# Query and key projections of two attentions: 512 weight columns a product, one norm for both

## Chip, cores and metric

One Trainium2 chip, one core. The metric is the time of one execution on the device, in microseconds (us), from three timed runs of the kernel before. The profile is of one further execution.

## What is computed

Two layers of a trunk, for 128 context tokens and 512 latent tokens that share all weights. In each layer a modulated RMS norm is followed by one input projection `z = h @ w_in` of 1024 features to 2560 columns, which are cut into eight parts:

```python
    lx, lg, nq, nk, nv, dq, dk, dv = in_projection(h, p['w_in'])      # 512, 512, then six of 256
    ya, sf, sb = lru_bidir(dwconv_centred(lx, ...), lg, p, zeros, zeros)
    q = rms_norm(nq.reshape(b, t, 4, 64), p['na_q_norm']) * 64 ** -0.5
    k = rms_norm(nk.reshape(b, t, 4, 64), p['na_k_norm'])
    q2 = rms_norm(dq.reshape(b, t, 4, 2, 32), p['df_q_norm'])
    k2 = rms_norm(dk.reshape(b, t, 4, 2, 32), p['df_k_norm'])
    y = jnp.concatenate([ya, merge_heads(yb), merge_heads(yc)], axis=-1) @ p['w_out']
```

`ya` is a bidirectional linear recurrence (LRU) on `lx`, gated by `lg`. `yb` is the neighbourhood attention (NA): 4 heads of 64, a window of 8 rows and 16 columns of the latent grid and 128 cached context keys; the context tokens attend among themselves. `yc` is the differential attention (DF): 4 heads of two components of 32, with rope on the latent tokens and cached keys as well. A norm over each head stands between projection and attention for all four of `nq`, `nk`, `dq`, `dk`. A convolutional feed-forward network closes the layer. Keys and values of the context tokens are outputs too.

## The kernel before, in words

All 640 tokens are handled at once: the modulated activations lie in `h`, features on partitions, as two tiles of rounded float32 (a high and a low part), and every weight is split in the same two parts on its way in. A product of two such numbers takes three matmuls: high by high, high by low, low by high (`mm3`, lines 269 to 274).

The weights pass three stations. `wload` (L361 to 365) brings 1 MB into one of two tiles of 2048 columns ("raw"), which the loads of the adaLN weights (`adaw`, 1 MB each, L196) share. `unit` (L372 to 378) splits half of it: ScalarE copies the high part (`wh`, L110), VectorE subtracts for the low part (`wl`, L117), 1024 columns each. The units lie in a ring of four (`ring`, L77), which the weights of the LRU (`lx` groups, and `gw0`) use first. A list `jobs` (L727 to 733) has the loads in order; `prep` (L735) does the next one, `take` (L739) hands out the oldest that is ready.

The attention projections have tokens on the output's partitions. `tok_chunk` (L817) takes one job of 8 x 256 weights, so two units, and goes over the five token tiles two at a time: a PSUM tile of 512 columns (`m`, three of them, L81) gets 256 columns for each of two token tiles, 24 products each. After the first two tiles it calls `prep` for the next chunk, and after each group one step of the adaLN generator `ada` (a load of 1 MB and four small products at L203). `normed_chunk` (L829) does so for a q or k: ScalarE copies the PSUM tile into `z` and squares it in place (L835), VectorE sums per head (L836). When all five tiles are through, `rsqrt` (L119) works out the inverse root by nine small VectorE operations behind two more, with 20 numbers a partition in NA and 40 in DF, and one multiplication scales `z` (L841).

The order in the program is `na_q`, `na_k`, the chunk of v, `na_prompt` and `na_sample` (attention of NA), `df_k`, `df_q`, the chunk of DF's v, then DF's scores (L1034 to 1048). `df_qk` (L891) adds gain and rope: four products on POOL (L905), a multiplication (L908) and a sum (L909) on VectorE. `df_k` then makes "stacks" of the keys (`stack`, L912): ScalarE and VectorE write high and low parts four times side by side, four transposes on TensorE (L920), copies into `ks`. DF's scores read these (L1079).

The order in which engines get their instructions is fixed when the program is built: a scheduler takes, at each simulated moment, the ready instruction of the best priority, which is its place in the program unless `later(n)` shifts it. It also gives out the buffers. Each engine then runs its own list in order and waits on semaphores. So a chunk of projections that stands behind `na_sample` in the program runs as filler while that waits for its softmax.

The job that a layer's mixer begins with is loaded earlier (`first`, L428 in layer 0, `job_load(l + 1)` at L1497 for layer 1).

Of the kernel before, what the change touches and what calls it, by code (L numbers as in the profile page):

```python
# [68 lines left out]
def trunk_kernel(ctx: ExitStack, tc: tile.TileContext, A, O):  # L69
# [26 lines left out]
    def m_tile():  # L96
        return ps_m.tile([P, 512], F32, tag="m", name="m")
# [10 lines left out]
    def copy(eng, out, in_):  # L108
        if eng == "a":
            return nc.scalar.activation(out, in_, AF.Copy)  # L110
        elif eng == "v":
            nc.vector.tensor_copy(out, in_)
        else:
            nc.gpsimd.tensor_copy(out, in_)
# [1 line left out]
    def sub(out, a, b, eng=None):  # L116
        (eng or nc.vector).tensor_tensor(out, a, b, op=OP.subtract)  # L117

    def rsqrt(v, n, name="rs"):  # L119
        yi = tiny.tile([P, max(n, 3)], I32, tag=f"yi{max(n, 3)}", name=name, bufs=2)[:, :n]  # L120
        nc.vector.tensor_scalar(yi, v.bitcast(I32), -0.5, float(0x5F3759DF), op0=OP.mult, op1=OP.add)
        y = yi.bitcast(F32)
        w = tiny.tile([P, max(n, 3)], F32, tag=f"yw{max(n, 3)}", name=name + "w", bufs=2)[:, :n]
        for _ in range(3):
            nc.vector.scalar_tensor_tensor(w, y, -0.5, y, op0=OP.mult, op1=OP.mult)
            nc.vector.tensor_tensor(w, w, v, op=OP.mult)
            nc.vector.scalar_tensor_tensor(y, w, 1.5, y, op0=OP.add, op1=OP.mult)
        return y
# [232 lines left out]
    def wload(src, off, row, nk, ncol):  # L361
        wl = raw_tile("w")
        nc.sync.dma_start(wl[:, :nk * ncol].rearrange("p (k c) -> p k c", k=nk),
                          dram(src, off, ((row, P), (P * row, nk), (1, ncol))))
        return wl

    def job_load(l):
        return wload(A["w_in"], l * D * D_IN + 1024, D_IN, 8, 256)

    split = []  # L370

# [125 lines left out]
    def wsplit(raw, nk, ncol, by_k=False, home=None, halves=False):  # L497
        raw = raw[:, :nk * ncol].rearrange("p (k c) -> p k c", k=nk)
        kk, cc = (nk // 2, ncol) if by_k else (nk, ncol // 2)
        parts = []  # L500

        def split_part():
            i = len(parts)
            parts.append(unit(raw[:, i * kk:i * kk + kk] if by_k else raw[:, :, i * cc:i * cc + cc], kk, home=home))
        split_part()
        if not halves:
            split_part()

        def get(k, c0, c1):
            i = k // kk if by_k else c0 // cc  # L510
            k, o = (k - i * kk, 0) if by_k else (k, i * cc)
            return tuple(w[:, k, c0 - o:c1 - o] for w in parts[i])
        return (get, split_part) if halves else get

    def weights(src, off, row, nk, ncol, by_k=False, home=None):
        return wsplit(wload(src, off, row, nk, ncol), nk, ncol, by_k, home)
# [80 lines left out]
    def mixer(xt, l, h, mix, ada, pre):  # L597
# [8 lines left out]
        def zb(name, dt=F32):  # L606
            return mix.tile([P, 2, T], dt, tag="zb", name=name, bufs=3)
# [7 lines left out]
        def heads(x, nh):  # L615
            return x.rearrange("p (h d) -> p h d", h=nh)

        def flat(x):
            return x.rearrange("p a b -> p (a b)")
# [104 lines left out]
                nc.vector.tensor_copy(nstate[:, l, dr, j:j + 1], th[:, dr, e:e + 1])  # L724
            nc.vector.tensor_tensor(glg[j], th[:, 0], th[:, 1], op=OP.add)

        jobs = [lambda: wsplit(first, 8, 256, True)]  # L727
        jobs += [lambda c=c: weights(A["w_in"], win + c, D_IN, 8, 256, True) for c in (1280, 1536, 2048, 1792, 2304)]
        jobs += [lambda jp=jp: weights(A["w_in"], win + 512 + jp * 256, D_IN, 8, 256) for jp in range(2)]
        jobs += [lambda cg=cg: weights(A["w_out"], wo + cg * 256, D, 6, 256) for cg in range(4)]  # L730
        jobs += [lambda: weights(A["w_out"], wo + 6 * P * D, D, 2, 1024, home=lambda n: flat(big(n, FR))),
# [7 lines left out]
        def take():  # L739
            if not ready:  # L740
                prep()
            return ready.pop(0)
# [74 lines left out]
        def tok_chunk(body):  # L817
            w = take()
            for t0, n in ((0, 2), (2, 2), (4, 1)):
                ps = m_tile()  # L820
                for t in range(t0, t0 + n):
                    c = (t - t0) * 256
                    mm3(ps[:, c:c + 256], [(cols(h, k, t * P, t * P + P), w(k, 0, 256)) for k in range(KD)])
                body(t0, n, ps[:, :n * 256])
                if t0 == 0:
                    prep()
                next(ada, None)

        def normed_chunk(nh, hd):  # L829
            z = flat(zb("z")).rearrange("p (t c) -> p t c", t=NT)  # L830
            v = tiny.tile([P, NT * nh], F32, tag=f"v{nh}", name="v", bufs=2)

            def body(t, n, ps):
                copy("a", flat(z[:, t:t + n]), ps)
                nc.scalar.activation(ps, ps, AF.Square)  # L835
                nc.vector.reduce_sum(v[:, t * nh:(t + n) * nh], heads(ps, n * nh), axis=AX.X)  # L836
            tok_chunk(body)
            nc.vector.tensor_scalar(v, v, 1.0 / hd, EPS, op0=OP.mult, op1=OP.add)
            r = rsqrt(v, NT * nh, "r")
            zv = z.rearrange("p t (h d) -> p (t h) d", h=nh)  # L840
            nc.vector.tensor_tensor(zv, zv, r[:, :, None].to_broadcast([P, NT * nh, hd]), op=OP.mult)  # L841
            return z

        def transpose2(z):
            pt = t_tile()
# [9 lines left out]
        gq = vec[l][:, V_GQ:V_GQ + 1]  # L855
        gk = vec[l][:, V_GK:V_GK + 1]

        def na_q():
            z = normed_chunk(4, 64)
            for t in range(NT):  # L860
                pt = transpose2(z[:, t])
                if t == 0:
                    nc.scalar.activation(qp, heads(pt, 2), AF.Copy, scale=gq)
                    continue
                i = t - 1
                for f in range(2):
                    o = qb[:, f, :, 6 - 2 * i:8 - 2 * i, :][:, :, ::-1, ::-1].rearrange("p b r c -> p r b c")
                    nc.scalar.activation(o, pt[:, f * P:f * P + P].rearrange("p (r b c) -> p r b c", r=2, b=4),
                                         AF.Copy, scale=gq)

        def na_k():
            z = normed_chunk(4, 64)
            ko = z_tile("ko")
            nc.vector.tensor_tensor(heads(ko, 4), heads(z[:, 0], 4), gna[:, None, :].to_broadcast([P, 4, 64]),
                                    op=OP.mult)
            out_cache("nk", ko, 4, 64)
            for t in range(NT):
                nc.scalar.activation(kt[:, :, t * P:t * P + P], heads(transpose2(z[:, t]), 2), AF.Copy, scale=gk)
# [9 lines left out]
                    copy("a", v, src)  # L888
                    nc.sync.dma_start(nvd[(t - 1) * P:t * P, :], v)

        def df_qk(w):  # L891
            z = normed_chunk(8, 32)
            z0 = heads(z[:, 0], 8)
            nc.vector.tensor_tensor(z0, z0, gdf[:, w][:, None, :].to_broadcast([P, 8, 32]), op=OP.mult)
            if w == 1:
                out_cache("dk", z[:, 0], 8, 32)
            tb = rope[w]
            zs = z[:, 1:]
            z2 = flat(zb("z2"))[:, :4 * 256].rearrange("p (t c) -> p t c", t=4)
            i6 = zs.rearrange("p t (h a e f) -> p t h a e f", h=8, a=2, e=2)  # L900
            o6 = z2.rearrange("p t (h a e f) -> p t h a e f", h=8, a=2, e=2)
            s5 = tb[:, 1].rearrange("p t (a e f) -> p t a e f", a=2, e=2)
            for a in range(2):
                for e in range(2):
                    nc.gpsimd.tensor_tensor(o6[:, :, :, a, e], i6[:, :, :, a, 1 - e],  # L905
                                            s5[:, :, None, a, e].to_broadcast([P, 4, 8, 8]), op=OP.mult)
            z4 = zs.rearrange("p t (h d) -> p t h d", h=8)
            nc.vector.tensor_tensor(z4, z4, tb[:, 0][:, :, None, :].to_broadcast([P, 4, 8, 32]), op=OP.mult)  # L908
            nc.vector.tensor_tensor(zs, zs, z2, op=OP.add)  # L909
            return z  # L910
# [10 lines left out]
                                    identr)  # L921
            return heads(pt, 4)

        def df_k():
            dkr = g_tile(256, name="dkr")
            nc.sync.dma_start(heads(dkr, 8), cache("cache_df_k", 8, 32))
            z = df_qk(1)
            copy("v", dkp, z[:, 0])
            ks = []
            for f in range(2):  # L930
                kf = [big("ks", FR) for _ in range(2)]
                for t in range(NT):
                    pt = stack((z[:, t + 1] if t < 4 else dkr)[:, f * P:f * P + P], True)
                    for i in range(2):
                        copy("av"[i], kf[i][:, :, t * P:t * P + P], pt[:, 2 * i:2 * i + 2])
                ks.append([kf[hc // 2][:, hc % 2] for hc in range(4)])
            return ks
# [93 lines left out]
                if g + 2 < 8:  # L1031
                    score(g + 2, head)

        na_q()  # L1034
        na_k()
        tok_chunk(na_v)
        if l == 0:
            for r in vecs_d(0):
# [2 lines left out]
        with later(400):  # L1041
            na_prompt()
        na_sample()
        ks = df_k()
        with later(-100):
            zq = df_qk(0)
        dv = flat(big("dv")).rearrange("p (t c) -> p t c", t=NT)
        tok_chunk(df_v)
        finish([ada])
# [503 lines left out]
```

## Time and profile before

| | us |
|---|---|
| median of the runs | 1601.61 |
| lowest and highest of three | 1600.32, 1602.11 |
| profiled execution | 1599.11 |
| its span, first to last instruction | 1597.3 |
| outside the span | 1.8 |

In the rows below a time is in us unless it says ns. PE is TensorE's matmul, PEld its weight load, DVE VectorE, ACT ScalarE, POOL GpSimd; "q" behind an engine is its queue of DMA issues. L272 is line 272 of the kernel; helpers like `copy` (L110) and `sub` (L117) have one line for all their callers, so one reads the names of the tiles as well. `m<-wh,h` is a product into an `m` tile with `wh` moving and `h` stationary, 128 x 128; `128x256` is the output. Durations of single matmuls overlap; their starts tell the pace.

### The profile page before, as it was taken

To read this page: it belongs to the slowest core of one execution; us is meant where nothing else is said; L and a number is where in the kernel's file an instruction comes from. 1 tells how busy PE (TensorE), PEld (TensorE's weight loads), DVE (VectorE), ACT (ScalarE), POOL (GpSimd) and SP (SyncE) were. 2 spreads that over 40 slices of the span, in tenths; PEclk is the share of its full clock that TensorE was granted. 3 is DMA by queue.
4 is the path that set the end of the run, shared out by engine and by line. 5 is a ranking of instruction groups with operands and counts; after the bars stand their busy time and mean duration, and the time that the engine had idled before them with its cause. 6 is when DMAs were issued, how large, how long until landed. Compare 5 with 4: busy or idle time off the path is not lost.

```text
span 1597.3 us, 28596 instructions
## 1 busy us (share of the span) xinstructions
PE 1552.9 (97%) x11183; PEld 1453.3 (91%) x11183; DVE 1321.2 (83%) x2894; ACT 917.2 (57%) x1689; POOL 89.9 (6%) x78
## 2 busy tenths in 40 slices
PE   7999999899999999999999899999999999999998
PEld 6877788799999999999998777988999999999998
DVE  5886778978999888888897776788799998888884
ACT  5865558746655454445458666685466554444451
POOL 0310200100000000000012201010000000000000
PEclk8999999999999999999999999999999999999999
DMA  9556632121444333222244564220312322222221
GB/s 329 182 196 219 174 108 87 47 80 37 142 153 137 99 89 89 80 77 73 90 145 132 185 215 126 70 106 29 89 54 73 116 80 80 80 80 80 73 73 67
DMA packets 208069, 177.30 MB, mean 111 GB/s; under 512 B 47574, under 2 KB 197310, under 8 KB 201790
## 3 DMA queue, kind: packets, MB, share of 16 engines
q1 hardware_dynamic: 207934, 175.48, 35.6%
q8 instruction: 88, 1.44, 0.4%
q14 instruction: 47, 0.39, 0.1%
HBM read 165.12 MB, written 10.34 MB: 110 GB/s over the span
## 4 chain that ended last, share of the span: by engine, by line
PE 78%; DVE 9%; ACT 5%; DMA 4%; issue 3%; POOL 1%; SPq 1%; DVEq 0%; ACTq 0%; POOLq 0%
PE m L283 6%; PE m L281 6%; PE m L282 6%; PE m L1286 6%; PE m L1287 6%; PE m L1288 5%; PE s L283 4%; PE s L282 4%; PE s L281 4%; PE m L272 3%; PE m L274 3%; PE m L273 3%; PE t L1288 3%; PE t L1286 3%; PE t L1287 3%
## 5 line engine op out<-in xcount | busy, mean ns | idle before, releaser
L117 DVE TENSOR_TENSOR wl<-up,wh 128x1024 fp32r<-128x1024 f32 x126 | 153.6, 1223 | 40.5 <-ACT wh L110 39.6
L110 ACT ACTIVATE wh<-up 128x1024 fp32r<-128x1024 f32 x126 | 132.2, 1052 | 81.6 <-PE t L1288 40.3
L1344 DVE SCALAR_TENSOR_TENSOR u<-raw,vec,u 128x127 f32<-128x127 f32 x352 | 175.4, 544 | 0.8 <-ACT u L1338 0.8
L272 PE MATMUL m<-wh,h 128*128 128x256 f32 x480 | 140.0, 292 | 0.0
L274 PE MATMUL m<-wh,h 128*128 128x256 f32 x480 | 138.2, 288 | 0.0
L273 PE MATMUL m<-wl,h 128*128 128x256 f32 x480 | 137.2, 286 | 0.0
L281 PE MATMUL m<-act,wh 128*128 128x320 f32 (+2 forms) x376 | 116.8, 311 | 0.0
L282 PE MATMUL m<-act,wl 128*128 128x320 f32 (+2 forms) x376 | 116.5, 310 | 0.0
L283 PE MATMUL m<-act,wh 128*128 128x320 f32 (+2 forms) x376 | 116.4, 310 | 0.0
L281 PE MATMUL s<-act,wh 128*128 128x320 f32 (+2 forms) x376 | 116.3, 309 | 0.0
L283 PE MATMUL s<-act,wh 128*128 128x320 f32 (+2 forms) x376 | 116.2, 309 | 0.0
L282 PE MATMUL s<-act,wl 128*128 128x320 f32 (+2 forms) x376 | 115.9, 309 | 0.0
L283 PE MATMUL m<-h,wh 128*128 128x320 f32 (+2 forms) x352 | 111.7, 319 | 2.9 <-DVE h L117 1.7
L281 PE MATMUL m<-h,wh 128*128 128x320 f32 (+2 forms) x352 | 111.3, 317 | 1.0 <-DVE xt L541 0.7
L282 PE MATMUL m<-h,wl 128*128 128x320 f32 (+2 forms) x352 | 110.9, 315 | 0.0
L541 DVE SCALAR_TENSOR_TENSOR xt<-m,mod,xt 128x128 f32<-128x128 f32 (+3 forms) x224 | 90.5, 432 | 16.7 <-PE m L283 15.8
L272 PEld LDWEIGHTS m<-wh,h 128*128 128x128 f32 x480 | 91.7, 191 | 12.9 <-issue 11.6
L274 PEld LDWEIGHTS m<-wh,h 128*128 128x128 f32 x480 | 91.6, 191 | 3.2 <-issue 2.7
L1286 PE MATMUL m<-h,wh 128*128 128x320 f32 x304 | 94.4, 311 | 0.0
L273 PEld LDWEIGHTS m<-wl,h 128*128 128x128 f32 x480 | 91.7, 191 | 2.9 <-issue 2.9
L1288 PE MATMUL t<-tx,wh 128*128 128x320 f32 x304 | 94.1, 310 | 0.0
L1286 PE MATMUL t<-tx,wh 128*128 128x320 f32 x304 | 94.1, 310 | 0.0
(371 smaller groups left out, 4948.9 us busy)
## 6 DMA issues: line engine op xcount, KB each, us to landing
up<-in_ffn_up_dram SPq DMA_DIRECT2D x88, 512.0 KB
adaw<-in_ada_w_dram SPq DMA_DIRECT2D x40, 1024.0 KB
w<-in_w_in_dram SPq DMA_DIRECT2D x16, 1024.0 KB
rawd<-in_ffn_down_dram SPq DMA_DIRECT2D x24, 512.0 KB
pro<-in_ada_w_dram SPq DMA_DIRECT2D x30, 256.0 KB
w<-in_w_out_dram SPq DMA_DIRECT2D x8, 768.0 KB
rawd<-in_ffn_down_dram SPq DMA_DIRECT2D x16, 384.0 KB
xd<-xt SPq DMA_DIRECT2D x4, 1280.0 KB
```

The source lines that it names most:

```text
L110: return nc.scalar.activation(out, in_, AF.Copy)
L117: (eng or nc.vector).tensor_tensor(out, a, b, op=OP.subtract)
L272: nc.tensor.matmul(out, st[0], mv[0], start=(i == 0), stop=False)
L273: nc.tensor.matmul(out, st[0], mv[1], start=False, stop=False)
L274: nc.tensor.matmul(out, st[1], mv[0], start=False, stop=(i == n - 1))
L281: nc.tensor.matmul(out, a[0], b[0], start=(k == total[0]), stop=False)
L282: nc.tensor.matmul(out, a[1], b[0], start=False, stop=False)
L283: last = nc.tensor.matmul(out, a[0], b[1], start=False, stop=(k == total[-1]))
L1286: nc.tensor.matmul(ps, st[0], mv[0], start=first and k == 0, stop=False, skip_group_check=chk)
L1287: nc.tensor.matmul(ps, st[1], mv[0], start=False, stop=False, skip_group_check=chk)
L1288: nc.tensor.matmul(ps, st[0], mv[1], start=False, stop=last and k == 3, skip_group_check=chk)
L1344: nc.vector.scalar_tensor_tensor(u[:, oa:ob], r[:, oa + sft:ob + sft], w, u[:, oa:ob], op0=OP.mult, op1=OP.add)
```

## The change

The two q and k columns of an attention, adjacent in `w_in`, are projected as one chunk of 512 columns. Its weights come as two jobs of 4 x 512 (k 0 to 3 and k 4 to 7), both taken before the first product, and `prep` for the next chunk stands in the last of the five token tiles. Each token tile has its own PSUM tile. ScalarE copies the two halves into two `z`, squares all 512 columns, VectorE sums for both. One `rsqrt` serves both (40 numbers in NA, 80 in DF); its tiles move to another pool. `na_q`, `na_k`, `df_k` and `df_qk` get their `z` handed in.

```diff
-    def job_load(l):
-        return wload(A["w_in"], l * D * D_IN + 1024, D_IN, 8, 256)
+    def job_load(l, kh=0, c=1024):
+        return wload(A["w_in"], (l * D + kh * 512) * D_IN + c, D_IN, 4, 512)
...
-        jobs = [lambda: wsplit(first, 8, 256, True)]
-        jobs += [lambda c=c: weights(A["w_in"], win + c, D_IN, 8, 256, True) for c in (1280, 1536, 2048, 1792, 2304)]
+        jobs = [lambda: wsplit(first, 4, 512, True), lambda: wsplit(job_load(l, 1), 4, 512, True)]
+        jobs += [lambda: weights(A["w_in"], win + 1536, D_IN, 8, 256, True)]
+        jobs += [lambda kh=kh: wsplit(job_load(l, kh, 1792), 4, 512, True) for kh in range(2)]
+        jobs += [lambda: weights(A["w_in"], win + 2304, D_IN, 8, 256, True)]
...
-        def normed_chunk(nh, hd):
-            z = flat(zb("z")).rearrange("p (t c) -> p t c", t=NT)
-            v = tiny.tile([P, NT * nh], F32, tag=f"v{nh}", name="v", bufs=2)
-
-            def body(t, n, ps):
-                copy("a", flat(z[:, t:t + n]), ps)
+        def tok_pair(body):
+            w = [take(), take()]
+            next(ada, None)
+            for t in range(NT):
+                ps = m_tile()
+                mm3(ps, [(cols(h, k, t * P, t * P + P), w[k // 4](k % 4, 0, 512)) for k in range(KD)])
+                if t == NT - 1:
+                    prep()
+                body(t, ps)
+                next(ada, None)
+
+        def normed_pair(nh, hd):
+            zs = [flat(zb("z")).rearrange("p (t c) -> p t c", t=NT) for i in range(2)]
+            n = 2 * nh
+            v = mix.tile([P, NT * n], F32, tag=f"v{n}", name="v", bufs=1)
+
+            def body(t, ps):
+                for i in range(2):
+                    copy("a", zs[i][:, t], ps[:, i * 256:i * 256 + 256])
                 nc.scalar.activation(ps, ps, AF.Square)
-                nc.vector.reduce_sum(v[:, t * nh:(t + n) * nh], heads(ps, n * nh), axis=AX.X)
-            tok_chunk(body)
+                nc.vector.reduce_sum(v[:, t * n:t * n + n], heads(ps, n), axis=AX.X)
+            tok_pair(body)
             nc.vector.tensor_scalar(v, v, 1.0 / hd, EPS, op0=OP.mult, op1=OP.add)
-            r = rsqrt(v, NT * nh, "r")
-            zv = z.rearrange("p t (h d) -> p (t h) d", h=nh)
-            nc.vector.tensor_tensor(zv, zv, r[:, :, None].to_broadcast([P, NT * nh, hd]), op=OP.mult)
-            return z
+            r = rsqrt(v, NT * n, "r", mix).rearrange("p (t h) -> p t h", t=NT)
+            for i, z in enumerate(zs):
+                zv = z.rearrange("p t (h d) -> p t h d", h=nh)
+                nc.vector.tensor_tensor(zv, zv, r[:, :, i * nh:i * nh + nh, None].to_broadcast([P, NT, nh, hd]), op=OP.mult)
+            return zs
...
-        na_q()
-        na_k()
+        zq, zk = normed_pair(4, 64)
+        na_q(zq)
+        na_k(zk)
         tok_chunk(na_v)
...
         na_sample()
-        ks = df_k()
+        zq, zk = normed_pair(8, 32)
+        ks = df_k(zk)
         with later(-100):
-            zq = df_qk(0)
+            df_qk(0, zq)
```

## Rows read from the trace of the kernel before

**Rows 1.** The profile page: busy time by engine, and the chain of waits.

```profile
PE 1552.9 (97%) x11183; PEld 1453.3 (91%) x11183; DVE 1321.2 (83%) x2894; ACT 917.2 (57%) x1689; POOL 89.9 (6%) x78
...
PE 78%; DVE 9%; ACT 5%; DMA 4%; issue 3%; POOL 1%; SPq 1%; DVEq 0%; ACTq 0%; POOLq 0%
```

**Rows 2.** Stretches: length, busy us (instructions) of PE, PEld, DVE, ACT, POOL; clock, DMA.

```profile
69.00:118.00 49.00, 46.91 (x352) 39.93 (x354) 42.21 (x77) 36.38 (x60) 13.86 (x10) 1.00 0.52 175
...
141.00:209.00 68.00, 63.74 (x528) 50.29 (x524) 41.06 (x118) 34.85 (x93) 9.54 (x13) 1.00 0.58 170
209.00:233.00 24.00, 23.96 (x205) 22.28 (x203) 17.46 (x40) 12.28 (x29) 3.16 (x4) 1.00 0.37 121
...
280.00:305.00 25.00, 20.55 (x133) 16.28 (x132) 23.81 (x81) 20.99 (x45) 7.48 (x4) 0.98 0.11 32
...
1063.00:1090.00 27.00, 22.23 (x146) 17.80 (x143) 25.44 (x87) 22.35 (x47) 7.91 (x4) 0.98 0.10 30
```

**Rows 3.** Instructions of line 272, the first of three products: ns least/median/most, starts.

```profile
L272 PEld LDWEIGHTS m<-wh,h x480: 186/192/246, 69.3 to 1011.6; 128*128 128x128 f32 x160
L272 PE MATMUL m<-wh,h x480: 276/283/388, 69.5 to 1011.7; 128*128 128x256 f32 x160
```

**Rows 4.** Timeline of TensorE, 256 columns: start, duration; seven steps apart.

```profile
76.36 0.28 PE L272 MATMUL m<-wh,h 128*128 128x256 f32 x1
...
77.20 0.28 PE L273 MATMUL m<-wl,h 128*128 128x256 f32 x1
```

**Rows 5.** Timeline of TensorE, 384 columns, six steps apart.

```profile
60.26 0.34 PE L281 MATMUL m<-h,wh 128*128 128x384 f32 x1
...
61.30 0.33 PE L281 MATMUL m<-h,wh 128*128 128x384 f32 x1
```

**Rows 6.** Timeline of TensorE, 320 columns, ten steps apart.

```profile
329.50 0.31 PE L282 MATMUL m<-h,wl 128*128 128x320 f32 x1
...
330.96 0.31 PE L283 MATMUL m<-h,wh 128*128 128x320 f32 x1
```

**Rows 7.** Waits of TensorE, 118 to 345 us: total, times, longest.

```profile
PE t L950 <- DVE p L957: 1.5, 1, 1.5
```

**Rows 8.** Groups by line and shape, 69 to 235 us: busy, mean ns, idle before.

```profile
L841 DVE TENSOR_TENSOR z<-z,r 128x1280 f32<-128x1280 f32 x4 | 6.0, 1488 | 0.1
L905 POOL TENSOR_TENSOR z<-z,rope 128x256 f32<-128x256 f32 x8 | 6.2, 799 | 27.5 <-DVE z L841 27.5
L908 DVE TENSOR_TENSOR z<-z,rope 128x1024 f32<-128x1024 f32 x2 | 2.5, 1225 | 2.6 <-POOL z L905 2.6
L909 DVE TENSOR_TENSOR z<-z,z 128x1024 f32<-128x1024 f32 x2 | 2.4, 1222 | 0.0
L126 DVE TENSOR_TENSOR rw<-rw,v 128x40 f32<-128x40 f32 x6 | 1.2, 197 | 0.2
L110 ACT ACTIVATE z<-m 128x512 f32<-128x512 f32 x8 | 4.7, 592 | 13.0 <-PE m L274 13.0
L110 ACT ACTIVATE z<-m 128x256 f32<-128x256 f32 x4 | 1.5, 380 | 1.7 <-PE m L274 1.7
```

**Rows 9.** The weights' tile w, 40 to 235 us: its splits, and waits for loads.

```profile
L110 ACT ACTIVATE wh<-w x16: 1041/1054/1072, 53.4 to 228.8; 128x1024 fp32r<-128x1024 f32 x16
L117 DVE TENSOR_TENSOR wl<-w,wh x16: 1212/1224/1311, 63.9 to 229.9; 128x1024 fp32r<-128x1024 f32 x16
...
  DMA w<-in_w_in_dram: 9.0, 4
```

**Rows 10.** Timelines: end of k's rope, q's last copy, first stack, first score.

```profile
180.77 1.22 DVE L909 TENSOR_TENSOR z<-z,z 128x1024 f32<-128x1024 f32 x1
...
208.99 0.37 ACT L110 ACTIVATE z<-m 128x256 f32<-128x256 f32 x1
...
209.04 0.53 PE L920 MATMUL t<-identr,st 128*128 128x128 f32 x4
...
232.81 0.44 PE L1079 MATMUL s<-kp,qs 128*128 128x128 f32 x2
```

More of the change, by code (lines that the diff above doesn't have):

```diff
@@ L117, in sub, with rsqrt @@
         (eng or nc.vector).tensor_tensor(out, a, b, op=OP.subtract)
-    def rsqrt(v, n, name="rs"):
-        yi = tiny.tile([P, max(n, 3)], I32, tag=f"yi{max(n, 3)}", name=name, bufs=2)[:, :n]
+    def rsqrt(v, n, name="rs", pool=tiny):
+        yi = pool.tile([P, max(n, 3)], I32, tag=f"yi{max(n, 3)}", name=name, bufs=2)[:, :n]
         nc.vector.tensor_scalar(yi, v.bitcast(I32), -0.5, float(0x5F3759DF), op0=OP.mult, op1=OP.add)
         y = yi.bitcast(F32)
-        w = tiny.tile([P, max(n, 3)], F32, tag=f"yw{max(n, 3)}", name=name + "w", bufs=2)[:, :n]
+        w = pool.tile([P, max(n, 3)], F32, tag=f"yw{max(n, 3)}", name=name + "w", bufs=2)[:, :n]
         for _ in range(3):
@@ L856, in mixer, with na_q @@
         gk = vec[l][:, V_GK:V_GK + 1]
-        def na_q():
-            z = normed_chunk(4, 64)
+        def na_q(z):
             for t in range(NT):
@@ L869, in na_q, with na_k @@
                                          AF.Copy, scale=gq)
-        def na_k():
-            z = normed_chunk(4, 64)
+        def na_k(z):
             ko = z_tile("ko")
@@ L889, in na_v, with df_qk @@
                     nc.sync.dma_start(nvd[(t - 1) * P:t * P, :], v)
-        def df_qk(w):
-            z = normed_chunk(8, 32)
+        def df_qk(w, z):
             z0 = heads(z[:, 0], 8)
@@ L922, in stack, with df_k @@
             return heads(pt, 4)
-        def df_k():
+        def df_k(z):
             dkr = g_tile(256, name="dkr")
             nc.sync.dma_start(heads(dkr, 8), cache("cache_df_k", 8, 32))
-            z = df_qk(1)
+            df_qk(1, z)
             copy("v", dkp, z[:, 0])
```

## The prediction

> **What bounds the kernel now.** I read the profile page first, then stretches of the two attention stages, then single instructions. The page has TensorE busy 97% of the span, VectorE 83%, ScalarE 57%, and a chain of waits that is 78% TensorE [rows 1]. Busy time of overlapping products is generous, so the stretches decide [rows 2]. While the q, k and v columns of the neighbourhood attention (NA) are projected (69 to 118 us), TensorE is busy 46.91 of 49 us; while NA runs with the q and k projections of the differential attention (DF) as filler (141 to 209), 63.74 of 68; while DF's keys are stacked and its first scores come (209 to 233), 23.96 of 24. Only at 280 to 305 us, and 1063 to 1090 in layer 1, is another engine the bound: VectorE 23.81 of 25 and 25.44 of 27 us, TensorE 20.55 and 22.23. The granted clock is 1.00, the 2.4 GHz level, where the changed projections stand. So they stand where TensorE's issue sets the pace, and their cost is the step from one product's start to the next, not the duration of one.
>
> **The products, removed and added.** Six projections to 256 columns make 480 groups of three products over two layers [rows 3]; four of the six change: 4 x 5 token tiles x 24 = 480 products of 256 columns a layer, 960 in all, become 240 and 480 of 512. Starts of 256-column products are 0.84 us apart over seven steps, 120 ns each [rows 4]; of 384 columns 1.04 us over six, 173.3 ns [rows 5]; of 320 columns 1.46 us over ten, 146 ns [rows 6]. The three lie on one line: 0.417 ns a column, one column a cycle at 2.4 GHz, and 13.3 ns a product whatever its width. At 512 columns the line gives 213.3 + 13.3 = 226.7 ns, against 240 for two of 256. **The gain is 480 x 13.3 ns = 6.4 us**, 3.2 a layer. No row has a 512-column product with 128 stationary columns, so bounds: with no fixed part at all on a wide product 480 x 26.7 = 12.8 us; with a doubled one, nothing. I take the line: 512 lies as far beyond 384 as 384 beyond 256, and 320 misses it by under 1 ns. A weight load lasts 192 ns [rows 3], and half as many are left, each beside 227 ns of product instead of 120, so loading cannot become the bound.
>
> In TensorE: Matmul & The Clock Gate, "Back-to-back issue gap", the Trainium skill gives a warm gap of columns / 2.4 plus 2.5 ns. That speaks against the change: by it the sum would be an estimated 480 x 2.5 ns = 1.2 us, which nobody could measure here. It also puts 256 columns at 109 ns, where rows 4 have 120, so the trace does not agree.
>
> **The head norms, computed together.** One chain of small VectorE operations with twice the elements replaces two. A 40-element step costs 197 ns [rows 8]; a chain has 11 steps (two scalings, three rounds of three), so 4 x 11 x 0.2 = 9 us leave VectorE. No 80-element step is in the trace; between the price of 40 and twice it, the two DF chains put 0 to 4.3 us back. I give the saving no time: at 141 to 209 VectorE is idle 27 of 68 us anyway. ScalarE's copies become ten of 256 columns a pair (380 ns) instead of six: four of 512 less (592) and eight of 256 more, 0.7 us longer; the squares become five instead of six. ScalarE is idle 12.6 of 49 us [rows 2], which hides it; without that cover 4 x 0.7 = 2.8 us. The broadcast multiplications stay two of 1280 elements. Each pair still issues two loads of 1 MB on SP's queue, and the next chunk's load is asked for in the pair's last tile instead of a chunk's first group, behind one adaLN load more.
>
> **The weights.** A pair needs four split units, and the ring has four. At the start, the pair's last two units wait for slots that the first LRU groups hold. The products of k 0 to 3 of three token tiles can run meanwhile, 36 x 0.227 = 8.2 us, for which there are three PSUM tiles; so nothing, and one split, 1.05 + 1.22 us [rows 9], if that cover is gone. At the end, the next chunk (v) can only be split as the pair's last tile lets units go: the first after 6 of 24 products, 4.1 us before the end, the second 2.7 us before it. A split takes 2.27 us, so it fits by 0.4 us if both engines take it at once and the load has landed. Before, ScalarE waited 9.0 us in four waits for such loads [rows 9], hidden behind a chunk whose weights lay ready; now nothing lies ready. Behind a late split are queued v's products, and behind those the next stage; adaLN's products and LRU gates can fill. So an end costs 0 to 2.27 us, more if the load is late. I take a quarter, near the lower end because the last tile (5.4 us) is longer than the split: 4 x 0.55 = **2.2 us**.
>
> **The DF keys, later.** Their norm and rope were done at 182 us, inside NA [rows 10], so the stacks began at 209, with q's projection barely ended; the first scores came at 232.8, behind q's own chain. Now k's chain follows the pair's end, at about 209 - 3.2 = 206. VectorE then has, beside what it did, the keys' multiplication, rope product and rope sum, 1.49 + 1.22 + 1.22 = 3.9 us [rows 8], and two splits of v, 2.4. It was idle 24 - 17.5 = 6.5 us there [rows 2]: just enough, and q's chain is no longer behind the stacks. I cost it at nothing; the other end is the last rival.
>
> **Sum.** 1599.1 us of the profiled execution - 6.4 + 2.2 = 1594.9. The median of the runs shown is 2.5 us above that execution, so **1597.4 us**. A measurement of this kernel can tell some 0.2%, 3.2 us, from no change.
>
> **Rivals.**
> The line holds, the ends are short (the forecast, 0.47): 1597.4, its own range 1591 to 1598.4. For it: inside a chunk the products follow each other without a gap, so what one saves moves everything behind it. Against: TensorE also waits for other engines' results, as 1.5 us on a softmax in NA [rows 7]; such waits take saved time back.
> Wide products gain little, so the change does not do what it says (0.11): the fixed part grows with the columns; 1600 to 1601.6, no change. The three points on one line speak against it. By the page's 2.5 ns it would be 1600.4, and that chance is within this one.
> Ring wait (0.20): every pair end pays a whole split, 4 x 2.27 = 9.1, less 6.4: 1604.3, within 0.2%. It decides from 1.6 us an end, which undoes the gain. For it: all four units are held; against: 4.1 us of warning.
> DF starts late (0.22): VectorE cannot hold the keys' chain and ten stacks before the first scores. The chain is serial: 11 small steps of 0.25, two multiplications 3.0, four POOL rope products 3.2, VectorE's rope 2.4, so 11.4 us from the pair's end to the first stack, where before there was nothing. v's chunk, 120 x 0.12 = 14.4 us, covers TensorE meanwhile, but is then missing under the stacks, and the later VectorE-bound stretch gives nothing back. If 8 of 11.4 us show in each layer: 16 - 6.4 = +9.6, 1611. It decides from 4.8 us a layer (9.6 - 6.4 = 3.2 slower); below 3.2 the sign stays mine.
>
> **Numbers.** Faster by over 0.2%: 0.47, the forecast. Same: 0.31, the second and third. Slower: 0.22, the last. The range runs from 1589.5, near the bound without a fixed part (1601.6 - 12.8 = 1588.8), to 1607, halfway into the last rival; about 0.1 lies above it and less below.
>
> **What would show it.** 512-column products starting 227 ns apart, and two chunks of 28.8 us become one of 27.2. At each pair end a TensorE gap under 1 us before v's first product; 2.3 for the ring. The first DF score 3 us earlier than 232.8; 5 us later is the last rival, with more TensorE idle time at 280 to 305. I am wrong if starts are 240 ns apart, or if TensorE's idle time between 69 and 345 us grows by more than 3 us a layer.

## The result, and the profile after

The changed kernel takes 1612.76 us (median of five runs, 1608.35 to 1615.84) against 1601.61: ratio 1.0067 (95% interval 1.0047 to 1.0088), **slower by 0.67%, some 11 us**. The profiled run took 1608.35 us, span 1606.6.

The page of after, busy time and chain of waits, answering to [rows 1]:

```profile
PE 1550.0 (96%) x10703; PEld 1421.1 (88%) x10703; DVE 1317.3 (82%) x2846; ACT 920.7 (57%) x1701; POOL 90.1 (6%) x78
...
PE 78%; DVE 11%; DMA 4%; ACT 4%; issue 2%; POOL 1%; SPq 0%; ACTq 0%; POOLq 0%; DVEq 0%
```

There are 480 products fewer, yet TensorE's busy time fell by only 2.9 us and the span grew by 9.3: its idle time is up by 12.2. The wide products themselves are as forecast. The timeline of TensorE in a pair's tile (start, duration), beside [rows 4]:

```profile
153.33 0.39 PE L272 MATMUL m<-wh,h 128*128 128x512 f32 x1
...
155.15 0.39 PE L274 MATMUL m<-wh,h 128*128 128x512 f32 x1
```

Eight steps in 1.82 us are 227.5 ns each; the line through the three widths gave 226.7.

Where the time went is read by following layer 0's milestones in after. First gate of LRU tile 2, first score of the neighbourhood attention (NA), its last values, first stack of keys, first score of the differential attention (DF), beside [rows 10]:

```profile
107.00 0.28 PE L272 MATMUL s<-xs,gh 128*128 128x256 f32 x1
...
164.55 0.37 PE L978 MATMUL s<-naset 64*128 64x128 f32 x1
...
219.00 0.88 PE L203 MATMUL t<-pT,naset 128*64 128x128 f32 x12
219.80 0.53 PE L933 MATMUL t<-identr,st 128*128 128x128 f32 x4
...
237.46 0.44 PE L1094 MATMUL s<-kp,qs 128*128 128x128 f32 x2
```

Before, that gate was at 90.0, the first NA score at 155.9, the last values at 208.2 and the first stack at 209.04. So NA starts 9 us later and ends 11 us later; the first DF score is 4.7 us late, and so is the end of the layer. Stretches of after (columns as in [rows 2]); 195 to 220 and 985 to 1010 are NA's last 25 us in the two layers:

```profile
69.00:118.00 49.00, 45.07 (x237) 32.09 (x236) 43.97 (x77) 32.16 (x54) 8.03 (x7) 1.00 0.59 189
118.00:141.00 23.00, 23.00 (x159) 18.99 (x157) 12.38 (x17) 19.08 (x30) 4.76 (x3) 0.94 0.57 182
141.00:209.00 68.00, 62.72 (x392) 42.08 (x389) 42.04 (x106) 33.69 (x90) 7.78 (x10) 0.97 0.61 185
195.00:220.00 25.00, 19.58 (x170) 15.58 (x170) 21.48 (x47) 14.45 (x40) 9.45 (x12) 0.93 0.59 165
220.00:241.00 21.00, 19.73 (x162) 18.49 (x162) 14.70 (x45) 13.46 (x36) 0.00 (x0) 1.00 0.14 45
...
285.00:310.00 25.00, 20.50 (x133) 16.26 (x132) 23.72 (x81) 21.02 (x45) 7.29 (x4) 0.97 0.11 32
985.00:1010.00 25.00, 17.99 (x171) 14.54 (x169) 21.22 (x47) 14.36 (x39) 9.39 (x12) 1.00 0.60 162
```

The same 25 us before NA's end in the kernel before:

```profile
184.00:209.00 25.00, 23.82 (x225) 18.93 (x223) 14.48 (x48) 16.40 (x48) 3.30 (x5) 1.00 0.53 138
968.00:993.00 25.00, 23.68 (x224) 18.76 (x222) 14.31 (x47) 16.61 (x49) 2.92 (x5) 1.00 0.52 135
```

TensorE loses 23.82 - 19.58 = 4.2 us in one layer and 5.7 in the other, while VectorE has 7 us **more** to do. At 285 to 310, the stretch in which VectorE was the bound, nothing changed (20.50 busy, 20.55 in [rows 2]). Inside NA's end, timelines of after on TensorE, VectorE and ScalarE, one fence each:

```profile
195.78 0.28 PE L274 MATMUL m<-wh,h 128*128 128x256 f32 x1
199.19 1.32 PE L203 MATMUL t<-pT,naset 128*64 128x128 f32 x12 [3.13 <-ACT pT L110]
```

```profile
193.88 0.24 DVE L125 SCALAR_TENSOR_TENSOR rw<-r 128x80 f32<-128x80 f32 x1
197.23 1.23 DVE L117 TENSOR_TENSOR wl<-w,wh 128x1024 fp32r<-128x1024 f32 x1 [3.11 <-ACT wh L110]
198.37 0.22 DVE L969 RECIPROCAL sm<-sm 128x1 f32<-128x1 f32 x2
```

```profile
196.14 1.06 ACT L110 ACTIVATE wh<-w 128x1024 fp32r<-128x1024 f32 x1 [4.13 <-DMA w<-in_w_in_dram]
197.10 0.60 ACT L968 ACTIVATE p<-p,nm 128x384 f32<-128x384 f32 x1
```

The DF pair is over at 190.5 us, 29 us before NA is. What follows a pair then stands in front of NA's softmax steps in the queues: the split of the job behind v's, the first `lg` columns (ScalarE waits 4.13 us for their load, NA's exponential behind it), on VectorE the norm and the split, and NA's reciprocal behind both. That load is the seventh of the layer in the order of `jobs`; v's, the sixth, went out at 164.26 us, and v's weights were split at 182.9 and 186.0, before the pair's end. The `lg` load went out when v's second split had freed a raw buffer. The queue of loads (SP) and that split on VectorE:

```profile
164.26 0.38 SPq L363 DMA_DIRECT2D w<-in_w_in_dram  x1
...
188.30 0.37 SPq L363 DMA_DIRECT2D w<-in_w_in_dram  x1
```

```profile
187.05 1.23 DVE L117 TENSOR_TENSOR wl<-w,wh 128x1024 fp32r<-128x1024 f32 x1 [0.32 <-ACT wh L110]
```

v's further products stand behind NA's in TensorE's own order. TensorE's waits in after, 60 to 345 us (total, times, longest):

```profile
PE t L203 <- ACT pT L110: 3.6, 2, 3.1
PE s L272 <- ACT r L658: 2.5, 1, 2.5
PE m L273 <- DVE wl L117: 2.1, 2, 1.4
PE t L963 <- DVE sm L969: 1.7, 2, 1.3
```

### The profile page after: what moved, and what is told of

It reads as the page before. It is cut to its first block, busy times and chain, and to the rows that moved or that the text cites. A ratio compares the mean times of both kernels' runs of the same rounds, so it can differ in the third digit from the quotient of the medians.

```text
span 1606.6 us, 27568 instructions
## 1 busy us (share of the span) xinstructions
PE 1550.0 (96%) x10703; PEld 1421.1 (88%) x10703; DVE 1317.3 (82%) x2846; ACT 920.7 (57%) x1701; POOL 90.1 (6%) x78
## 4 chain that ended last, share of the span: by engine, by line
PE 78%; DVE 11%; DMA 4%; ACT 4%; issue 2%; POOL 1%; SPq 0%; ACTq 0%; POOLq 0%; DVEq 0%
PE m L283 6%; PE m L281 6%; PE m L282 6%; PE m L1301 5%; PE m L1302 5%; PE m L1303 5%; PE s L281 4%; PE s L283 4%; PE s L282 4%; PE m L274 3%; PE m L273 3%; PE m L272 3%; PE t L1303 3%; PE t L1302 3%; PE t L1301 3%
## 5 line engine op out<-in xcount | busy, mean ns | idle before, releaser
L273 PE MATMUL m<-wl,h 128*128 128x512 f32 (+1 forms) x320 | 110.9, 347 | 3.0 <-DVE wl L117 2.8
L272 PE MATMUL m<-wh,h 128*128 128x512 f32 (+1 forms) x320 | 111.4, 351 | 0.0
L274 PE MATMUL m<-wh,h 128*128 128x512 f32 (+1 forms) x320 | 111.2, 348 | 0.0
L1301 PE MATMUL m<-h,wh 128*128 128x320 f32 x304 | 94.4, 310 | 0.5 <-ACT wh L110 0.5
L1302 PE MATMUL t<-tx,wl 128*128 128x320 f32 x304 | 93.9, 309 | 0.0
L1302 PE MATMUL m<-h,wl 128*128 128x320 f32 x304 | 93.9, 309 | 0.0
L1303 PE MATMUL m<-h,wh 128*128 128x320 f32 x304 | 93.9, 309 | 0.0
```

The lines of the kernel that those rows point to most:

```text
L272: nc.tensor.matmul(out, st[0], mv[0], start=(i == 0), stop=False)
L273: nc.tensor.matmul(out, st[0], mv[1], start=False, stop=False)
L274: nc.tensor.matmul(out, st[1], mv[0], start=False, stop=(i == n - 1))
L1301: nc.tensor.matmul(ps, st[0], mv[0], start=first and k == 0, stop=False, skip_group_check=chk)
L1302: nc.tensor.matmul(ps, st[1], mv[0], start=False, stop=False, skip_group_check=chk)
L1303: nc.tensor.matmul(ps, st[0], mv[1], start=False, stop=last and k == 3, skip_group_check=chk)
```

## The experiments

Ratios are to the kernel before, with 95% intervals. Theory A: the order of work shifted, because a distance such as `later(300)` counts instructions, and half as many products make it last longer. Theory B: weights come late at a pair's end. Theory C: the DF keys are late, the last rival on record.

### Which part, and which theory

The counter moved on, so that a wide product takes two places (nothing that is computed changes):

```diff
                 mm3(ps, [(cols(h, k, t * P, t * P + P), w[k // 4](k % 4, 0, 512)) for k in range(KD)])
+                tc.cur_priority += 24
```

> After each token tile of a pair the scheduler's place counter goes 24 further, so that a pair of 24 wide products a tile takes up as many places as the 48 products it replaces; nothing that is computed changes. Theory A (places): the scheduler orders by place in the program, the distances such as 300 for the gates of LRU tiles 2 and 3 count instructions, and half as many products make them last nearly twice as long, so the gates came 17 us later, the neighbourhood attention (NA) 11 us later, and its filler ran out before its end. It expects the first such gate near 90 us again (after: 107), NA's last value near 209 to 212 us (after: 219.6) and 1598 to 1603 us. Theory B (late weights): the loss is that at a pair's end the next weights are loaded and split with nothing in store; this edit leaves that, so 1610 to 1614 us. Theory C (late DF keys, the last rival on record): also untouched, 1610 to 1614.

Measured: 1600.46 us, 0.9994 (0.9981 to 1.0008). The loss is gone. The first gate came at 96.5, not near 90.

The same places with narrow products:

```diff
-                mm3(ps, [(cols(h, k, t * P, t * P + P), w[k // 4](k % 4, 0, 512)) for k in range(KD)])
+                for c in (0, 256):
+                    mm3(ps[:, c:c + 256], [(cols(h, k, t * P, t * P + P), w[k // 4](k % 4, c, c + 256)) for k in range(KD)])
```

> A pair's 512-column products are written as two of 256 each, in the pair's order (weights, norms and copies as after); so 960 products and the places of before. Theory A: places as in the run with the counter moved on, and 480 x 13.3 ns = 6.4 us more than that run: 1604 to 1609 us, under the 1612.8 of after although its products are dearer. Theory B: after plus 6.4 us, 1619. Theory C: 1619 too. If the two runs of this pair differ by under 2 us, the gain of a wide product is not what its start times say.

Measured: 1618.52 us, 1.0107 (1.0080 to 1.0134), 18 us above the run before it where 6.4 were expected. The first stack came at 227.6 us, with 218.8 there. Theory A had the size wrong here; the last two runs below return to it.

One attention at a time (the other keeps its two chunks and norms of before):

```diff
-        zq, zk = normed_pair(8, 32)
-        ks = df_k(zk)
+        ks = df_k(normed_chunk(8, 32))
         with later(-100):
-            df_qk(0, zq)
+            zq = df_qk(0, normed_chunk(8, 32))
```

> Only NA has the pair; the differential attention (DF) has its two 256-column chunks with their own norms, as before. Theory A: the gates and NA are late as after, so most of the loss stays: 1606 to 1611 us, first gate of tile 2 near 107 us. Theory B: one of two pair ends a layer, half of the loss, about 1606. Theory C: DF's keys are early again, so the time is that of before less 3.2 us, 1598.

Measured: 1599.21 us, 0.9986 (0.9971 to 1.0002), though the first gate was at 107.3. Theory A's expectation missed: late gates cost nothing to speak of.

```diff
-        zq, zk = normed_pair(4, 64)
-        na_q(zq)
-        na_k(zk)
+        na_q(normed_chunk(4, 64))
+        na_k(normed_chunk(4, 64))
```

> Only DF has the pair; NA has its chunks of 256 columns as before. Theory A: gates and NA start as before (first gate of tile 2 at 90 us), so the loss is small: 1598 to 1603 us, before less 3.2 plus what the weights cost. Theory B: half of the loss, about 1606 us. Theory C: the whole loss, 1611 to 1615 us, with the first DF score 5 us late.

Measured: 1611.83 us, 1.0072 (1.0046 to 1.0097). **The whole loss sits in the DF pair**, with gates as before. NA's end in this run has the same hole as after (stretches, columns as above):

```profile
195.00:220.00 25.00, 20.83 (x183) 16.43 (x175) 21.65 (x50) 14.36 (x39) 9.53 (x12) 0.93 0.63 170
985.00:1010.00 25.00, 18.58 (x175) 14.95 (x173) 21.72 (x48) 14.64 (x40) 9.58 (x12) 1.00 0.59 162
```

In the run with the counter moved on, the same 25 us before NA's end:

```profile
176.00:201.00 25.00, 24.93 (x201) 18.55 (x200) 15.20 (x44) 16.26 (x45) 4.29 (x6) 1.00 0.52 139
960.00:985.00 25.00, 24.91 (x207) 18.60 (x205) 15.07 (x44) 16.62 (x45) 4.27 (x6) 1.00 0.53 139
```

TensorE is full and VectorE back at 15: the pair's last product starts at 201.45 us, NA's last values at 199.84.

### The distance alone, and the weights

```diff
-        with later(400):
+        with later(370):
             na_prompt()
```

> The kernel after, with one number changed: the prompt block of the neighbourhood attention (NA) stands 370 places later than its place, not 400. Theory A, narrowed by the first runs (the NA pair alone cost nothing though its gates came 17 us late; the DF pair alone cost all): the 400 places are passed by the DF pair's products, each now twice as long, so three token tiles of the pair run ahead of NA's first scores where two narrow groups did; NA then starts and ends about 10 us late, and its end has no products left to fill it. It expects NA's first sample score near 164 us (after: 173), its last value near 205 to 212, and 1598 to 1604 us. Theory B (late weights) and theory C (late DF keys): unchanged or worse, 1610 to 1614 us.

> As the run with 370, with 350 places. Theory A: NA is ahead by another 5 us; what was lost stays won, and what the earlier NA leaves for its end (the pair's own key chain, theory C) begins to show: 1598 to 1606 us. Theory B: 1610 to 1614.

Measured: 1611.0 us, 1.0047 (1.0032 to 1.0063) with 370; 1605.84 us, 1.0023 (1.0010 to 1.0035) with 350. NA ended at 210 and 203 us as theory A had it, but the time was won back in part only: the pair now ended late, at 205.5 and 204.1 us, with 350 after NA, the first stacks came at 224.0 and 221.2 us, and TensorE was busy 15.15 and 17.33 of 20 us at 220 to 240. Theory C's wait is real once NA is out of the way.

```diff
-        with later(400):
+        with later(460):
             na_prompt()
```

> The kernel before, with the prompt block of NA 460 places later, not 400: no product, weight or norm is touched. Theory A: the same loss without the change: NA's first sample score near 173 us (before: 162), its last value near 219, and 1605 to 1612 us. Theories B and C: 1600 to 1603 us, since nothing they speak of is changed.

Measured (kernel before with this line): 1602.24 us, 0.9993 (0.9983 to 1.0003). **Theory A falls in this form.** NA's first score at 166.5 us is as late as after, and nothing is lost. The 25 us before its end, layer 0 and 1:

```profile
190.00:215.00 25.00, 22.68 (x205) 17.84 (x205) 20.00 (x60) 16.33 (x46) 7.77 (x10) 1.00 0.69 185
974.00:999.00 25.00, 21.96 (x199) 17.25 (x201) 20.91 (x61) 16.15 (x45) 7.80 (x10) 1.00 0.67 177
```

VectorE is loaded here too, and TensorE loses 1.1 and 1.7 us, not 4.2 and 5.7; the time is that of before. A late NA is not enough; theory A2 was formed: what costs is that the pair, keys and queries at once, is used up inside NA.

```diff
+                if t == 2:
+                    held.append(wload(A["w_in"], win + c, D_IN, 8, 256))
```

> The kernel after, with the load (not the split) of the v chunk's weights asked for in a pair's third token tile, not its last. Theory B: ScalarE's waits of 2.65 and 4.13 us on these loads in layer 0 go, and with them what stood behind them, two of this size a layer: 1600 to 1605 us. Theory A: the order stays, NA is as late, and TensorE has as little to fill its end: 1609 to 1613 us.

Measured: 1610.29 us, 1.0051 (1.0034 to 1.0068), which cannot be told from after. v's load in the DF pair went out at 156.54 us, not 164.26. But the wait of 4.13 us was not on v's weights: it stayed, 3.80 us, and so did TensorE's hole behind it (2.77 us; after: 3.13). The queue of loads and ScalarE in this run:

```profile
188.04 0.37 SPq L363 DMA_DIRECT2D w<-in_w_in_dram  x1
```

```profile
195.51 1.06 ACT L110 ACTIVATE wh<-w 128x1024 fp32r<-128x1024 f32 x1 [3.80 <-DMA w<-in_w_in_dram]
```

This is the `lg` load, which the edit does not move. So theory B falls for v's weights; for the job behind them it was not tested.

### Which pair's places, and the norms

The line with `tc.cur_priority += 24` for the NA pair alone, then for the DF pair alone:

> The place counter moves on by 24 a token tile in the pair of the neighbourhood attention (NA) alone; the pair of the differential attention (DF) counts as after. Theory A2 (the run of before with 460 places showed that a late NA alone costs nothing): what costs is that the DF pair is used up inside NA, about 27 us before NA ends, so that NA's last groups stand alone with TensorE while the weights of v, the norms and the rope of both z pass through ScalarE and VectorE in front of their softmax. In this kernel's order NA still stands as late against the DF pair as after, so 1609 to 1614 us, though its gates are early again. Theory G (late gates cost): 1600 to 1603.

> The counter moves on by 24 in the DF pair alone; the NA pair counts as after, and its gates stay at 107 us. Theory A2: the DF pair lasts until NA's end again (its last product after 195 us, NA's last value near 203), so most of the loss is won back: 1600 to 1605 us. Theory G: 1609 to 1613.

Measured: 1607.12 us, 1.0031 (1.0017 to 1.0044), and 1608.48, 1.0037 (1.0024 to 1.0050). Neither wins all, the two together do; A2 expected nothing of the first and nearly all of the second. In the first, NA's end has the hole of after (7.01 busy of 10 us at 195 to 205; after: 6.87), while the gate's wait of 2.5 us on ScalarE's r is gone; why early gates gain something here, and next to nothing with the NA pair alone, stays open. In the second NA ended at 204, but the stacks began at 222.2, and TensorE was busy 16.41 of 20 us at 220 to 240, at a granted clock of 0.74.

The wide products kept, the head norms apart:

```diff
-            r = rsqrt(v, NT * n, "r", mix).rearrange("p (t h) -> p t h", t=NT)
+            def norm(i):
...
+                r = rsqrt(vi, NT * nh, "r")
...
-        zq, zk = normed_pair(8, 32)
-        ks = df_k(zk)
+        norm = normed_pair(8, 32)
+        ks = df_k(norm(1))
         with later(-100):
-            df_qk(0, zq)
+            zq = df_qk(0, norm(0))
```

> The wide products of after with the head norms apart again: after a pair each of the two z has its own chain of small steps and its own multiplication, the second one where it stood before. Theory D (the joint norm is the part that costs: both chains must pass VectorE at once, in front of NA's last softmax steps): 1602 to 1607 us. Theory A2: the order of products and NA stays that of after, and the second chain only moves a few us; VectorE's waits shrink a little: 1607 to 1613 us.

Measured: 1616.16 us, 1.0089 (1.0064 to 1.0114). Theory D falls: the joint norm is not what costs.

The NA pair alone, with the counter moved on by 24:

> The NA pair alone (DF in its two chunks of 256 columns as before), with the counter moved on by 24 a tile: the best kernel by theory A2, since NA's pair gains 3.2 us and DF's filler stays in two parts, keys early and queries to the end of NA. It expects 1596 to 1600 us; against the run with the NA pair alone (0.9986 of before) the early gates give at most 2 us more. If it is over 1602, the counter itself costs.

Measured: 1598.72 us, 0.9979 (0.9967 to 0.9992).

### What was still open

The DF pair alone with the counter moved on:

> The run with the DF pair alone (1611.8 us, the whole loss), with the place counter moved on by 24 a tile of that pair; NA's chunks and gates are those of before. Theory A2 (the pair used up inside NA, whose end then stands alone): NA ends near 203 us with pair products beside it to the end, 1600 to 1604 us. Theory C (the late keys by themselves): the stacks of keys begin near 220 us as they did (220.0), and with the pair's end later nothing can be won, 1608 to 1613 us.

Measured: 1603.29 us, 1.0010 (0.9996 to 1.0024), 8.5 us under the run without it. How the counter does it is seen by counting products from NA's z transposes to its first score. Instructions of line 272, a third of the products (count; least, median, most ns; first and last start), first without it, then with it:

```profile
L272 PE MATMUL m<-wh,h x24: 387/391/500, 142.1 to 163.9; 128*128 128x512 f32 x24
```

```profile
L272 PE MATMUL m<-wh,h x16: 388/389/474, 141.9 to 156.6; 128*128 128x512 f32 x16
```

Three token tiles of the pair run ahead of NA without it, two with it. Before, it was 95 narrow products, four tiles of 256 columns, over by 155.9.

The kernel before, counted short:

```diff
-        def tok_chunk(body):
+        def tok_chunk(body, less=0):
...
+                tc.cur_priority -= less * n
...
-            tok_chunk(body)
+            tok_chunk(body, 12)
```

> The kernel before, with the place counter taken back by 12 a token tile of each query or key chunk, so that the projections take up as many places as the pairs do in the kernel after; no product, weight or norm is changed. If shorter places are enough for the loss by themselves: 1608 to 1613 us. Theory A2: the gates come about 12 us later and NA as late as in the run with 460 places, but keys and queries are still two chunks with the keys early and the queries to the end of NA, so little is lost: 1601 to 1605 us.

Measured: 1603.18 us, 1.0009 (0.9995 to 1.0023). Short places without pairs cost 1.5 us, by the interval 3.7 at most; so it takes both, **the shorter places and keys and queries in one pair**, as A2 says.

Norms apart, with the counter moved on:

> The wide products with the head norms apart, and the counter moved on by 24 a tile in both pairs: beside the run with the counter alone (1600.5 us) it differs in the norms only. If computing them together saves time in the right order: 1602 to 1606 us, since in each pair one chain of ten small VectorE steps of 0.2 us more stands before the stacks or NA. If it saves none, as costed on record: 1599 to 1602.

Measured: 1611.96 us, 1.0064 (1.0039 to 1.0090), 11 us above the joint norms in the same places, not 2 to 6. The first DF score on a long key block is 3.3 us later. At 280 to 290, 290 to 300 and 300 to 310 us the granted clock was 0.88, 0.78 and 0.74, and 1.00 in the run with joint norms; these 30 us alone are an estimated 1.2 + 2.2 + 2.6 = 6.0 us. The clock over whole runs was 0.985 as against 0.991, an estimated 10 of the 11 us at most (1612 x 0.006, as if TensorE set the pace throughout). So little of the difference need be the time of the norm steps; why the clock fell, no run shows.

The counter moved on, and the early load of v:

> The counter moved on by 24 in both pairs, and the v chunk's load asked for in the pair's third tile. Theory A2 with the weights as a small second term (after, the earlier load gave 2.5 us, within the noise): 1597 to 1600 us, as good as the NA pair alone. If the loads cost nothing once the order is right: 1599 to 1602 us, and the load holds one of the two raw buffers longer, so adaLN's loads may take 1 to 2 us back.

Measured: 1600.51 us, 0.9991 (0.9977 to 1.0005), the same as without the early load. v's load in the DF pair went out at 158.96 us, not 174.37; ScalarE's waits for the `lg` load, 1.51 and 3.02 us in the two layers, are those without it (1.49 and 3.02).

The wide product by itself, in the NA pair alone, whose end no stack waits for; narrow, then wide:

> The NA pair alone, its 512-column products written as two of 256 (480 in place of 240 over both layers, counted as 48 places a tile by themselves); DF's chunks as before. Against the kernel run beside it, which differs in these products alone, 240 x 13.3 ns = 3.2 us more by the price on record: about 1601.9 where that has 1598.7. If a wide product's price differs by what it does to the order, as the 18 us between the first two runs say: over 8 us more, 1607 or above. If wide products gain nothing: the same time within 1.5 us.

> The NA pair alone with the counter moved on by 24, the same kernel as the run of 1598.7 us, once more beside the run with 256-column products, and to narrow its interval (0.9967 to 0.9992): 1597 to 1600 us, ratio 0.997 to 0.999.

Measured: 1601.60 us, 0.9990 (0.9978 to 1.0002), and 1599.28, 0.9973 (0.9960 to 0.9986). The difference is 0.0017, or 2.7 us, against 3.2 from the start times; the two intervals overlap, the scatter of the runs leaves some 0.5 to 5 us, and 8 us are excluded. So the product itself is not what the 18 us above were. Of them 6.4 are its price on both pairs, and the granted clock over whole runs, 0.984 with narrow products as against 0.991 with wide ones, is an estimated 11 at most (1618 x 0.007); why it was lower was not tested. **The wide one of these two is the best kernel found, 0.21% and 0.27% faster than before in its two measurements; it beats the kernels before and after.**

## Why the prediction was wrong

**The products were right.** 227 ns a step were forecast and measured; for one pair 3.2 us were forecast and 2.7 appear in the time, loosely (0.5 to 5). The gap that remains between wide products is 227.5 - 213.3 = 14 ns. The Trainium skill, in TensorE: Matmul & The Clock Gate, "Back-to-back issue gap", gives 2.5 ns, as the gap of a single product and not of a stream of weight loads and products; in the stream here, the trace does not agree at 512 columns either.

**The step that failed** is "Now k's chain follows the pair's end, at about 209 - 3.2 = 206", and with it "I cost it at nothing". It took the pair's end from the place of q's last copy before, and so took over the order of work around the change. But the same diff halves the count of instructions by which that order is made. Three token tiles of the pair ran ahead of NA, the pair ended at 190.5, and its norms, ropes and the weights of the job behind v's fell into NA's end, where VectorE had 7 us more to do and TensorE lost 4.2 and 5.7 us. These 9.9 us outweigh the 6.4 gained; 1.3 us at 220 to 241, where before none stood, are a further term. The gates' wait of 2.5 us is none by itself: between 69 and 195 us TensorE stood idle 5.1 us after and 5.5 before. A term that neither the prediction nor the theories had is the granted clock: 0.94 at 118 to 141 us and 0.93 at 195 to 220, both 1.00 before, an estimated 1.4 + 1.8 = 3.2 us. Layer 0 then comes to an estimated 4.2 + 1.3 + 3.2 - 3.2 = 5.5 us, where its first DF score was 4.7 late. The sign of being wrong that the prediction named came: from 69 to 345 us TensorE's idle time grew from 11.3 to 16.4 us, by more than 3. Before, then after:

```profile
69.00:345.00 276.00, 264.73 (x2048) 226.98 (x2047) 217.23 (x588) 182.72 (x398) 36.61 (x32) 0.99 0.40 127
```

```profile
69.00:345.00 276.00, 259.61 (x1772) 207.48 (x1771) 209.01 (x553) 181.49 (x399) 34.28 (x31) 0.98 0.40 125
```

**The last rival had the time, 1611, but not the mechanism.** It set the loss between the pair's end and the first stack; after, the first stack follows NA's last values without a gap. Its mark, a first DF score 5 us late, came (4.7), its other one, more idle time at 280 to 305, did not. The wait that it described is what the runs show where the order is mended: with the counter moved on, the first stack of layer 0 on the timeline of TensorE is this:

```profile
218.82 0.51 PE L934 MATMUL t<-identr,st 128*128 128x128 f32 x4 [2.50 <-DVE st L117]
```

There it is paid for by NA's full end, and the sum comes to about nothing, 1600.5.

**The weights** of v were in time, as the prediction had it: in layer 0's DF pair they were split before the pair's end, and their load asked for earlier changed nothing that can be told from noise, in either order. What its term leaves out is the job behind them. ScalarE waited 4.13 and 4.05 us for the `lg` load in the two layers, and TensorE's holes of 3.13 and 3.05 us, 6.2 of the 9.9, stand right behind these waits; the prediction has 0.55 us an end. With the counter moved on, the `lg` load goes out at 199.47 us, when NA is all but over, and ScalarE's wait for it opens no hole in NA.

**The head norms** were costed right as instructions: a scaling of 80 elements took 199 ns, the integer step 202 and the nine steps behind them 240 where nothing slowed them, as against 183, 184 and 200 of 40 elements in the same trace, so a joint chain lasts about a fifth longer than one chain, and the two DF chains put back an estimated 0.8 us of "0 to 4.3". "I give the saving no time" did not hold once the order was mended: there, the kernel with separate norms took 11 us more, most of which may be its lower clock. In the order of after the 3.4 us between the two cannot be told from noise.

What was not separated: which of the things that the pair brings into NA's end (the norms, the ropes, the late `lg` weights) takes how much of the 9.9 us; no run moves the `lg` load or its split by itself. What lowers the clock in one order of work and not in another is open too, though it is worth an estimated 11 us at most between kernels here.

## What to carry to other kernels

Where the order of work is made from counts of instructions, a change that halves a count moves everything that is placed by distance; before costing an edit, ask what the order is keyed to, and give the new instruction the places of the old ones. Two products that filled another stage one after the other are not the same filler when they are joined: both results then come at once, early or late, and what hangs on each has to be placed anew. Mend the order before judging such a change: in the one attention where nothing hung on the first half, the wide products and joint norms were worth 0.2 to 0.3%. And read the granted clock of every run beside its time before calling the difference the price of an edit.

## What the hardware showed unexpectedly

A hole in TensorE's work can cost more than its length, but does not always. In layer 0 of after, behind 3.13 us without a product, twelve small products took 1.32 us and the granted clock of the next 5 us was 0.71, between the levels of 1.2 and 2.4 GHz; in layer 1 the same hole and the same products:

```profile
989.44 0.88 PE L203 MATMUL t<-pT,naset 128*64 128x128 f32 x12 [3.05 <-ACT pT L110]
```

They took 0.88 us, and the clock stayed at 1.00. What decides between the two, no run here shows.
